# Hybrid recurrent decoder step: projections as one plain fp32 matmul per 128 rows in place of three float32r products

## The chip, the cores and the metric

The kernel runs on one core of one Trainium2 chip. The metric is the device time of one execution in microseconds (us); lower is better. A core has five engines that run their own queues in order: PE (TensorE, matmuls; its weight loads are listed apart as PEld), DVE (VectorE), ACT (ScalarE), POOL (GpSimd) and SP (SyncE), which here issues the DMAs.

## The reference

One layer (model width 1024) serves a prompt of 1024 tokens and eight sample sequences of one token each. What matters here are the two large projections around the mixers:

```python
h = rms_norm(x, norm_g)
proj = jnp.matmul(h, w_in).astype(F32)       # 1032 rows, 30 tiles of 128 columns
...                                          # GLA, S5, gated delta net, RWKV-7, each times a SiLU gate
mixed = jnp.concatenate([o_gla, o_s5, o_gdn, o_rwkv], axis=-1)
out = jnp.matmul(mixed, w_out.astype(F32))   # 1032 rows, 8 tiles of 128 columns
return x + out.astype(x.dtype), ...
```

The final RMSNorm follows. The mixers are recurrences over the tokens, worked out in chunks; the projected columns feed them, and all of it is float32.

## The kernel before

The tokens are handled in two halves: 512 prompt tokens (half 0), and 512 prompt tokens with the 8 sample tokens (half 1, 520 columns in two pieces of 260). `norm_x` normalizes the rows of a half, transposes them on PE and keeps them as two float32r tiles: `xhi`, the rounded value, and `xlo`, what the rounding left. `stream` computes 128 projected columns: eight weight slabs of 128x128 are brought in two transfers into `wr`, and `wsplit` makes the same two parts of them, `wh` on ACT (L265) and `wl` on POOL (L266). Then each slab is multiplied three times into one PSUM tile `psp` (L277): `xhi` by `wh`, `xlo` by `wh`, `xhi` by `wl`. A caller's `evac` takes `psp` away on ACT or DVE. `proj` calls `stream` for the 30 input tiles of each half; `tail` does so for the 8 output tiles (L277 with `ohi` and `olo`), then transposes (L1301), adds x (L1303) and normalizes.

The work between is that of the units named in a list `ORDER`: RWKV (R, chain of chunk states at L483), gated delta net (D, chain at L689), GLA (L, L819), S5 (W for its block matrices, S), and gates (g). The inverses that R and D need are a chain of 31 pairs of small DVE operations (L307, L309). L1184 is the one other large weight product, of S5's gate (`yt` by `wglu`), in plain float32. A scheduler sets the order on every engine from `ORDER` and a table of priorities, so that projections stand in PE's queue between the steps of the recurrences. Raw weights have three buffers, `wh` and `wl` two each; `xhi` and `xlo` (and `ohi`, `olo`, which use the same space) have one.

Of the kernel before, what the change touches and what calls it, by code (L numbers as in the profile page):

```python
# [9 lines left out]
F32R = mybir.dt.float32r  # L10
# [6 lines left out]
T = 1024  # L17
# [7 lines left out]
NB = dict(ta=9, pr=11, on=3, gp=8, sh=2, kA=6, XT=2, Gt=5, s8=4, ss=4, wr=3, wh=2, wl=2, d1=1, LT=1, DT=2, DP=1, d2=2, Dn=2, w8=2, rf=1,  # L25
# [5 lines left out]
           rU="V", dU="V", fg="V", la="V", tlo="V", cv0="V")  # L31
# [32 lines left out]
def trunk(ctx: ExitStack, tc: tile.TileContext, I, O):  # L64
# [20 lines left out]
    def cload(name, shape):  # L85
        """A block of columns of the constants that one transfer brings."""
        b, o, p = CONST[name]
        if b not in blobs:
            blobs[b] = const.tile([128, CONST_W[b]], F32, name="const" + b)
            SP.dma_start(out=blobs[b], in_=I["const" + b])  # L90
        v = blobs[b][:p, o:o + math.prod(shape[1:])]
        return v.rearrange("p (a b) -> p a b", a=shape[1]) if len(shape) == 3 else v

    def late(ins, after):
        """Schedule ins, which nothing else holds back, only when after has been issued: its tile waits for its turn."""
# [18 lines left out]
    def tt(name, out, a, b, op=ALU.mult):  # L114
        """out = a op b on the engine that ENG names."""
# [14 lines left out]
    def load_x(h, after=None):  # L130
        """The rows of a half and the gains of its norm."""
# [11 lines left out]
    # ------------------------------------------------------------ constants  # L143
# [29 lines left out]
    # what is carried from the first half of the sequence to the second  # L173
# [12 lines left out]
    # ------------------------------------------------------------ small pieces  # L186
    def rsqrt_small(y, m, t):
        """y = m ** -0.5 for small tiles: ln and exp, then a Newton step."""
# [7 lines left out]
    def sig_arg(e, x, bias=None):  # L196
        """e = x (+ bias), bounded where exp(-x) would run out of the range of Ln: 1 / (1 + e^43) < 2^-62."""
# [5 lines left out]
    def sig_chain(e, *outs):  # L203
        """sigmoid(e) to each (out, columns of e)."""
# [8 lines left out]
    def sample_bc(src):  # L213
        """[128 (h, v), 8] -> PSUM [128 (h, any), 8, 64]: each head's values along the free dim."""
# [6 lines left out]
    def mat_vec(S, col):  # L221
        """sum over keys i of S[(h, i), b, v] * col[(h, i), b], on all partitions of the head."""
# [13 lines left out]
    # ------------------------------------------------------------ projection stream  # L236
    def norm_x(h, tiles):
        """RMSNorm of a half, transposed, in two parts that float32r holds exactly."""
        hi = xp.tile([128, 8, NH], F32R, tag="hi", name="xhi")
        lo = xp.tile([128, 8, NH], F32R, tag="lo", name="xlo")  # L240
        ngb = tiles[0]
        for i in range(5 if h else 4):
# [9 lines left out]
            for b in range(2):  # L252
# [3 lines left out]
                A.copy(hi[:, 4 * b:4 * b + 4, c:c + n], pt[:, :, :n])  # L256
                V.tensor_tensor(lo[:, 4 * b:4 * b + 4, c:c + n], pt[:, :, :n], hi[:, 4 * b:4 * b + 4, c:c + n], ALU.subtract)  # L257
        XS[h] = dict(hi=hi, lo=lo, n=NH if h else HALF)

    def wsplit(src):  # L260
        raw = wst.tile([128, 4, 128], F32, tag="wr", bufs=NB["wr"], name="wr")
        SP.dma_start(out=raw, in_=src)
        hi = wst.tile([128, 4, 128], F32R, tag="wh", bufs=NB["wh"], name="wh")
        lo = wst.tile([128, 4, 128], F32R, tag="wl", bufs=NB["wl"], name="wl")
        A.copy(hi, raw)  # L265
        G.tensor_tensor(lo, raw, hi, ALU.subtract)  # L266
        return hi, lo

    def stream(wsrc, evac):
        """evac(PSUM [128, m], c0, m) for the columns of (128 columns of w).T @ x."""  # L270
        wt = [wsplit(wsrc[:, 4 * q:4 * q + 4, :]) for q in range(2)]
        for c0, m in X["pieces"] or pieces(X["n"]):
            p = ps_p.tile([128, 512], F32, tag="p", name="psp")
            for k in range(8):
                hi, lo = wt[k // 4]
                for s, (w, x) in enumerate(((hi, X["hi"]), (hi, X["lo"]), (lo, X["hi"]))):
                    X["mm"] = PE.matmul(p[:, :m], w[:, k % 4, :], x[:, k, c0:c0 + m], start=(k == 0 and s == 0), stop=(k == 7 and s == 2))  # L277
# [8 lines left out]
    # ------------------------------------------------------------ inverses of unit lower triangular matrices  # L286
    def inverse(Ga, XT, after):
        """XT[64 p + s, k, t] = ((I - L) ** -1)[t, s] for the 16 strictly lower L[t, s] = Ga[p][..][s, k, t] of a unit;
        p is the parity of a chunk and k = (pair of chunks, head), in one or two tiles."""
# [39 lines left out]
    # pairs of chunks are kept as (first of one, second of one, second of the other, first of the other)  # L329
# [10 lines left out]
    # ------------------------------------------------------------ RWKV-7  # L340
# [164 lines left out]
    # ------------------------------------------------------------ gated delta net  # L505
# [10 lines left out]
    def small_in(h):  # L516
        """low-rank gate of GLA (rows 0:16), a (32:36) and b (64:68) of the delta net."""
# [56 lines left out]
    def conv_in(h, ct, raw):  # L574
        """causal convolution over 4 tokens and SiLU of one column tile of q, k, v."""
# [25 lines left out]
    def l2(x, out, scale, eps):  # L601
        """out = x * (scale * (sum over the head of x * x) + eps) ** -0.5"""
# [105 lines left out]
    # ------------------------------------------------------------ gated linear attention  # L708
# [6 lines left out]
    def gla_unit(h, pair, sm):  # L715
# [55 lines left out]
        # q.k of a token with itself, and of the second of two with the first, by rows of the first  # L771
# [738 lines left out]
```

## Time and profile before

| | |
|---|---|
| three runs | 1075.30, 1083.88, 1084.38 us; median 1083.88 |
| profiled execution, first to last instruction (span) | 1069.0 us |
| PE busy | 928.3 us, 87% of the span, 5994 matmul records |
| DVE busy | 704.2 us, 66% |
| ACT busy | 459.6 us, 43% |
| POOL busy | 395.3 us, 37% |
| mean granted clock of PE | 0.858 of full speed |

The page gives the span of the profiled execution and no time of its own beside it; the three runs lie 6.3 to 15.4 us above that span. Busy time is the time in which at least one record of an engine runs. Matmul records overlap, so the pace of a stream is read from the starts of its records, not from their durations. A plain float32 matmul of full width leaves two records, a float32r one leaves one.

### The profile page before, as it was taken

How to read it: one execution, taken by the hardware profiler on the slowest of the kernel's cores; microseconds unless marked ns; L12 is line 12 of the kernel's file. 1: busy time of each engine (PE TensorE's matmuls, PEld its weight loads, DVE VectorE, ACT ScalarE, POOL GpSimd, SP SyncE). 2: the span in 40 equal slices, each digit the busy share in tenths (PEclk: the TensorE clock that was granted, in tenths of full speed). 3: DMA queues.
4: the chain of work that ended last, by engine and by line, in shares of the span. 5: the costliest groups of instructions: out<-in, count | busy, mean ns of one | idle time of the engine just before them, and what ended most of it. 6: DMA issues, size and time to landing. Idle time of an engine off the chain costs nothing. (4 is left out here: it accounts for less than half of the span.)

```text
span 1069.0 us, 16993 instructions
## 1 busy us (share of the span) xinstructions
PE 928.3 (87%) x5994; PEld 762.7 (71%) x5994; DVE 704.2 (66%) x1871; ACT 459.6 (43%) x1033; POOL 395.3 (37%) x434
## 2 busy tenths in 40 slices
PE   3899889979999788897989898988989989769794
PEld 3676657658777576797788767677868958658694
DVE  8528884668648864736578989979875366553514
ACT  4355544332644343522753454643235235162634
POOL 2788654531321441133363403125326312313231
PEclk9999979876898666798999889888888569869898
DMA  7133414210211132224223223311112014612532
GB/s 235 50 127 106 115 59 111 71 54 21 74 49 43 46 93 81 81 79 148 69 85 97 77 76 83 92 47 50 53 59 71 22 66 126 212 49 79 183 128 86
DMA packets 76804, 92.23 MB, mean 86 GB/s; under 512 B 41400, under 2 KB 43584, under 8 KB 76720
## 3 DMA queue, kind: packets, MB, share of 16 engines
q1 hardware_dynamic: 76720, 91.16, 27.2%
q8 instruction: 47, 0.77, 0.3%
q14 instruction: 37, 0.30, 0.1%
HBM read 74.38 MB, written 14.62 MB: 83 GB/s over the span
## 5 line engine op out<-in xcount | busy, mean ns | idle before, releaser
L266 POOL TENSOR_TENSOR wl<-wr,wh 128x512 fp32r<-128x512 f32 x152 | 204.6, 1348 | 420.5 <-ACT wh L265 403.6
L277 PE MATMUL psp<-xhi,wh 128*128 128x260 f32 (+2 forms) x728 | 262.2, 361 | 10.7 <-DVE rx L355 6.5
L277 PE MATMUL psp<-xhi,wl 128*128 128x260 f32 (+2 forms) x728 | 256.3, 355 | 5.2 <-POOL wl L266 5.0
L277 PE MATMUL psp<-xlo,wh 128*128 128x260 f32 (+2 forms) x728 | 253.3, 349 | 0.8 <-DVE xlo L257 0.8
L277 PEld LDWEIGHTS psp<-xhi,wh 128*128 128x128 f32 x728 | 153.2, 210 | 33.8 <-issue 12.8
L277 PEld LDWEIGHTS psp<-xhi,wl 128*128 128x128 f32 x728 | 151.2, 209 | 25.4 <-POOL wl L266 7.4
L265 ACT CAST wh<-wr 128x512 fp32r<-128x512 f32 x152 | 93.7, 618 | 172.3 <-PE psp L277 92.9
L277 PEld LDWEIGHTS psp<-xlo,wh 128*128 128x128 f32 x728 | 153.2, 211 | 16.7 <-issue 3.8
L307 DVE TENSOR_TENSOR DP<-DT,LT 128x60 f32<-128x60 f32 (+24 forms) x248 | 81.9, 330 | 12.5 <-DMA XT<-d 3.1
L309 DVE TENSOR_TENSOR DT<-DT,DP 128x60 f32<-128x60 f32 (+24 forms) x248 | 73.8, 297 | 6.1
L277 PE MATMUL psp<-ohi,wh 128*128 128x260 f32 (+1 forms) x192 | 65.5, 342 | 5.4 <-ACT yT L1295 3.5
L277 PE MATMUL psp<-olo,wh 128*128 128x260 f32 (+1 forms) x192 | 64.0, 334 | 1.8 <-DVE olo L116 1.8
L277 PE MATMUL psp<-ohi,wl 128*128 128x260 f32 (+1 forms) x192 | 62.9, 334 | 0.0
L1303 DVE TENSOR_TENSOR xf<-psb,xf 128x128 f32<-128x128 f32 x64 | 14.5, 282 | 49.6 <-PE psb L1301 41.3
L277 PEld LDWEIGHTS psp<-ohi,wh 128*128 128x128 f32 x192 | 37.7, 197 | 8.5 <-ACT yT L1295 3.9
L762 PE MATMUL psb<-W 64*128 64x64 f32 x256 | 40.7, 331 | 1.8 <-DVE DT L309 1.8
L112 ACT ACTIVATE eg<-eg 128x260 f32<-128x260 f32 (+1 forms) x72 | 34.0, 486 | 18.2 <-DVE eg L199 17.4
L277 PEld LDWEIGHTS psp<-olo,wh 128*128 128x128 f32 x192 | 37.7, 196 | 4.6 <-DVE olo L116 2.1
L762 PEld LDWEIGHTS psb<-W 64*128 64x128 f32 x256 | 36.4, 237 | 5.7 <-issue 3.1
L277 PEld LDWEIGHTS psp<-ohi,wl 128*128 128x128 f32 x192 | 37.0, 195 | 2.4 <-POOL wl L266 0.2
L116 POOL TENSOR_TENSOR df<-cum 128x256 f32<-128x256 f32 x48 | 30.8, 663 | 17.2 <-DVE cum L737 15.2
L483 PE MATMUL psc<-UV,Gt 64*128 64x64 f32 (+1 forms) x256 | 35.6, 288 | 0.6 <-ACT UV L476 0.6
(423 smaller groups left out, 1862.4 us busy)
## 6 DMA issues: line engine op xcount, KB each, us to landing
wr<-in_wct SPq DMA_DIRECT2D x120, 256.0 KB
wr<-in_wo SPq DMA_DIRECT2D x32, 256.0 KB
xn<-in_x SPq DMA_DIRECT2D x8, 512.0 KB
LT<-d SPq DMA_DIRECT2D x32, 128.0 KB
xf<-in_x SPq DMA_DIRECT2D x8, 512.0 KB
out_y<-xf SPq DMA_DIRECT2D x8, 512.0 KB
dgp<-gp SPq DMA_DIRECT2D x8, 256.0 KB
Gml<-dG SPq DMA_DIRECT2D x4, 512.0 KB
```

The lines of the kernel that those rows point to most:

```text
L112: A.activation(out, in_, func, bias=bias, scale=scale, **kw)
L116: return (G if ENG[name] == "G" else V).tensor_tensor(out, a, b, op)
L265: A.copy(hi, raw)
L266: G.tensor_tensor(lo, raw, hi, ALU.subtract)
L277: X["mm"] = PE.matmul(p[:, :m], w[:, k % 4, :], x[:, k, c0:c0 + m], start=(k == 0 and s == 0), stop=(k == 7 and s == 2))
L307: V.tensor_tensor(tp[:, :m, :w], DT[:, :m, j:j + 1].to_broadcast([128, m, w]), LT[:, j:j + 1, j + 1:32].to_broadcast([128, m, w]), ALU.mult)
L309: V.tensor_tensor(DT[:, :m, j + 1:32], DT[:, :m, j + 1:32], tp[:, :m, :w], ALU.add)
L483: PE.matmul(o, l, r, start=start, stop=True, skip_group_check=True)
L762: PE.matmul(pg[:, c, :], W[HS[e], t], W[HS[e], t].rearrange("p (b f s) -> p f b s", f=2, s=s)[:, 1], start=True, stop=True)
L1303: V.tensor_tensor(xf[j][:, cols], pt[:, j, :], xf[j][:, cols], ALU.add)
```

## The change

The split is taken out everywhere. `norm_x` writes the transposed rows once, as float32 (`xT`); `wload` brings the weights and PE reads them where they land; `stream` makes one float32 matmul per slab (L268 in the changed kernel, where lines stand 9 to 11 earlier). `tail` copies half 1's gates into one float32 tile `oT`, and loads half 0's there by DMA directly. Raw weights get six buffers, and `xT`/`oT` two. All other lines of the difference are comments.

```diff
-NB = dict(..., wr=3, wh=2, wl=2, ...
+NB = dict(..., wr=6, xT=2, ...
...
     def norm_x(h, tiles):
-        hi = xp.tile([128, 8, NH], F32R, tag="hi", name="xhi")
-        lo = xp.tile([128, 8, NH], F32R, tag="lo", name="xlo")
+        xt_ = xp.tile([128, 8, NH], F32, tag="x", bufs=NB["xT"], name="xT")
...
-                A.copy(hi[:, 4 * b:4 * b + 4, c:c + n], pt[:, :, :n])
-                V.tensor_tensor(lo[:, 4 * b:4 * b + 4, c:c + n], pt[:, :, :n], hi[:, 4 * b:4 * b + 4, c:c + n], ALU.subtract)
-        XS[h] = dict(hi=hi, lo=lo, n=NH if h else HALF)
-
-    def wsplit(src):
-        raw = wst.tile([128, 4, 128], F32, tag="wr", bufs=NB["wr"], name="wr")
-        SP.dma_start(out=raw, in_=src)
-        hi = wst.tile([128, 4, 128], F32R, tag="wh", bufs=NB["wh"], name="wh")
-        lo = wst.tile([128, 4, 128], F32R, tag="wl", bufs=NB["wl"], name="wl")
-        A.copy(hi, raw)
-        G.tensor_tensor(lo, raw, hi, ALU.subtract)
-        return hi, lo
+                A.copy(xt_[:, 4 * b:4 * b + 4, c:c + n], pt[:, :, :n])
+        XS[h] = dict(x=xt_, n=NH if h else HALF)
+
+    def wload(src):
+        w = wst.tile([128, 4, 128], F32, tag="wr", bufs=NB["wr"], name="wr")
+        SP.dma_start(out=w, in_=src)
+        return w
...
             for k in range(8):
-                hi, lo = wt[k // 4]
-                for s, (w, x) in enumerate(((hi, X["hi"]), (hi, X["lo"]), (lo, X["hi"]))):
-                    X["mm"] = PE.matmul(p[:, :m], w[:, k % 4, :], x[:, k, c0:c0 + m], start=(k == 0 and s == 0), stop=(k == 7 and s == 2))
+                X["mm"] = PE.matmul(p[:, :m], wt[k // 4][:, k % 4, :], X["x"][:, k, c0:c0 + m], start=(k == 0), stop=(k == 7))
...
     def tail(h):
-        hi = xp.tile([128, 8, NH], F32R, tag="hi", name="ohi")
-        lo = xp.tile([128, 8, NH], F32R, tag="lo", name="olo")
+        ot = xp.tile([128, 8, NH], F32, tag="x", bufs=NB["xT"], name="oT")
...
-            if not h:
-                p = prt("gpl")
-                SP.dma_start(out=p[:, :n], in_=dgp[k])
-            A.copy(hi[:, k, :n], p[:, :n])
-            tt("tlo", lo[:, k, :n], p[:, :n], hi[:, k, :n], ALU.subtract)
-        X.update(hi=hi, lo=lo, n=n)
+            if h:
+                A.copy(ot[:, k, :n], p[:, :n])
+            else:
+                SP.dma_start(out=ot[:, k, :n], in_=dgp[k])
+        X.update(x=ot, n=n)
```

The scheduler writes a new order for every engine. Three places show it. The first is ACT's queue at the start of half 0, before:

```order
L256 CAST xhi<-psb 128x4x128 x2
L112 ACTIVATE ss<-ss 128x1 x2
L265 CAST wh<-wr 128x512 x2
L256 CAST xhi<-psb 128x4x128 x4
L112 ACTIVATE sh<-psp,constA 128x256
```

and after:

```order
L254 COPY xT<-psb 128x4x128 x2
L111 ACTIVATE ss<-ss 128x1 x2
L254 COPY xT<-psb 128x4x128 x2
L111 ACTIVATE sh<-psp,constA 128x256
L254 COPY xT<-psb 128x4x128 x4
```

The casts of weights (`wh`) are gone, and the first evacuation of a projection (`sh`, from `psp`) stands ahead of the last four copies.

The second is PE's queue among the first chunk steps of an RWKV chain in half 0 (`UV`, `Gt`, `Bn`, `AR`, `XT` and `state` are the chain's tiles), before:

```order
L277 MATMUL psp<-xlo,wh 128x512
L277 MATMUL psp<-xhi,wl 128x512
L277 MATMUL psp<-xhi,wh 128x512
L728 MATMUL psb<-sm,constB 128x512
L483 MATMUL psc<-UV,Bn 128x128
L483 MATMUL psc<-UV,Gt 64x64 x2
```

and after:

```order
L474 MATMUL psc<-r,XT 64x64 x2
L474 MATMUL psc<-UV,Gt 128x64 x4
L474 MATMUL psc<-UV,Bn 128x128
L474 MATMUL psc<-UV,Gt 64x64 x2
L474 MATMUL psc<-state_116,AR 128x128
L461 MATMUL psc<-constA,BK 128x128 x2
```

Projections that stood between the first chunk steps now stand elsewhere: there is no L268 among them.

The third is PE's queue in the last output tiles of half 1, before:

```order
L277 MATMUL psp<-olo,wh 128x260
L1301 MATMUL psb<-constA,yT 128x128 x2
L1306 MATMUL psb<-constA,yT 8x128
L277 MATMUL psp<-ohi,wh 128x260
L277 MATMUL psp<-olo,wh 128x260
L277 MATMUL psp<-ohi,wl 128x260
```

and after:

```order
L268 MATMUL psp<-oT,wr 128x260 x12
L1290 MATMUL psb<-constA,yT 128x128 x2
L268 MATMUL psp<-oT,wr 128x260 x4
L1290 MATMUL psb<-constA,yT 128x128 x2
L1295 MATMUL psb<-constA,yT 8x128
```

The transposes of one tile still stand among the products of the next; 16 float32 matmuls now make a tile, where 48 float32r ones did.

## Rows read from the trace of the kernel before

**Rows 1.** The page, part 1: busy time, share of the span and records.

```profile
PE 928.3 (87%) x5994; PEld 762.7 (71%) x5994; DVE 704.2 (66%) x1871; ACT 459.6 (43%) x1033; POOL 395.3 (37%) x434
```

**Rows 2.** Windows by stage: length, busy time per engine, granted clock, DMA share, GB/s.

```profile
27.00:200.00 173.00, 157.37 (x760) 113.96 (x759) 105.64 (x230) 77.23 (x147) 111.19 (x122) 0.90 0.30 93
200.00:460.00 260.00, 229.65 (x1434) 182.29 (x1433) 176.42 (x497) 107.86 (x250) 76.72 (x85) 0.78 0.20 63
460.00:600.00 140.00, 124.79 (x891) 111.82 (x890) 94.76 (x191) 63.68 (x133) 60.48 (x74) 0.95 0.30 92
600.00:918.00 318.00, 290.96 (x2123) 243.38 (x2122) 239.25 (x645) 135.84 (x336) 98.43 (x100) 0.85 0.23 69
952.00:1050.00 98.00, 90.84 (x578) 81.19 (x579) 40.42 (x136) 37.98 (x87) 34.45 (x26) 0.94 0.31 111
```

**Rows 3.** Waits of PE: who waited for whom, us in total, times, longest.

```profile
PE psc L689 <- DVE U L122: 9.2, 7, 2.6
PE psb L255 <- DVE xlo L257: 9.1, 5, 4.2
PE psp L277 <- POOL wl L266: 5.0, 5, 2.9
```

**Rows 4.** Groups by line and shape: count, busy us, mean ns, idle before.

```profile
L266 POOL TENSOR_TENSOR wl<-wr,wh 128x512 fp32r<-128x512 f32 x152 | 204.6, 1348 | 420.5 <-ACT wh L265 403.6 <-PE psp L277 13.1 <-PE psb L1086 2.1
L277 PE MATMUL psp<-xhi,wh 128*128 128x260 f32 x480 | 153.2, 320 | 8.3 <-DVE rx L355 6.5 <-DVE gp L1218 1.0 <-ACT shout L359 0.8
L277 PEld LDWEIGHTS psp<-xhi,wh 128*128 128x128 f32 x728 | 153.2, 210 | 33.8 <-issue 12.8 <-DVE gp L1218 3.7 <-ACT wh L265 3.0
L277 PE MATMUL psp<-xhi,wh 128*128 128x512 f32 x232 | 103.6, 446 | 2.4 <-ACT wh L265 1.5 <-DVE gp L1218 0.9
L265 ACT CAST wh<-wr 128x512 fp32r<-128x512 f32 x152 | 93.7, 618 | 172.3 <-PE psp L277 92.9 <-issue 66.8 <-POOL sh L350 5.9
L277 PE MATMUL psp<-ohi,wh 128*128 128x260 f32 x128 | 38.2, 300 | 2.0 <-ACT ohi L1266 2.0
L277 PE MATMUL psp<-ohi,wh 128*128 128x512 f32 x64 | 27.3, 426 | 3.5 <-ACT yT L1295 3.5
```

**Rows 5.** Timeline of PE, float32r projections: start us, us; first and last of a run.

```profile
58.94 0.39 PE L277 MATMUL psp<-xlo,wh 128*128 128x512 f32 x1
...
60.80 0.40 PE L277 MATMUL psp<-xhi,wh 128*128 128x512 f32 x1
...
518.71 0.29 PE L277 MATMUL psp<-xhi,wl 128*128 128x260 f32 x1
...
519.66 0.28 PE L277 MATMUL psp<-xlo,wh 128*128 128x260 f32 x1
...
702.35 0.42 PE L277 MATMUL psp<-xlo,wh 128*128 128x260 f32 x1
...
703.87 0.42 PE L277 MATMUL psp<-xhi,wl 128*128 128x260 f32 x1
```

**Rows 6.** Line L1184, plain float32: its records, and two merged stretches of the timeline.

```profile
L1184 PE MATMUL psb<-yt,wglu x24: 382/592/803, 519.8 to 948.0; 128*128 128x260 f32 x16, 128*128 128x512 f32 x8
...
519.79 1.45 PE L1184 MATMUL psb<-yt,wglu 128*128 128x512 f32 x3
...
947.08 1.26 PE L1184 MATMUL psb<-yt,wglu 128*128 128x260 f32 x5
```

**Rows 7.** The inverses on DVE: duration min/median/max of L307, and its group on the page.

```profile
L307 DVE TENSOR_TENSOR DP<-DT,LT x248: 136/220/1317, 119.6 to 757.7; 128x60 f32<-128x60 f32 x12, 128x54 f32<-128x54 f32 x8, 128x66 f32<-128x66 f32 x8, 128x28 f32<-128x28 f32 x8
...
L307 DVE TENSOR_TENSOR DP<-DT,LT 128x60 f32<-128x60 f32 (+24 forms) x248 | 81.9, 330 | 12.5 <-DMA XT<-d 3.1
```

More of the change, by code (lines that the diff above doesn't have):

```diff
@@ L9 @@
 F32 = mybir.dt.float32
-F32R = mybir.dt.float32r
 I32 = mybir.dt.int32
@@ L24 @@
 NH = HALF + NS
-NB = dict(ta=9, pr=11, on=3, gp=8, sh=2, kA=6, XT=2, Gt=5, s8=4, ss=4, wr=3, wh=2, wl=2, d1=1, LT=1, DT=2, DP=1, d2=2, Dn=2, w8=2, rf=1,
+NB = dict(ta=9, pr=11, on=3, gp=8, sh=2, kA=6, XT=2, Gt=5, s8=4, ss=4, wr=6, xT=2, d1=1, LT=1, DT=2, DP=1, d2=2, Dn=2, w8=2, rf=1,
           fx=3, bv=2, Bn=2, UV=2, r=3, dr=2, gcn=2, ben=2, kdn=2, U=3, at=2, s5i=1, s5h=3, nst=2, psp=2, psb=2, psc=4)
@@ L30 @@
            glu="V", g5="V", cvm="V", l2="V", sgl1="V", sgl2="V", lw0="V", lw1="G", ld0="G", ld1="G", lqk="V", rS="A", rr="V",
-           rU="V", dU="V", fg="V", la="V", tlo="V", cv0="V")
+           rU="V", dU="V", fg="V", la="V", cv0="V")
 PRI = {"R2": 4000, "D2": 1000, "R3": 4000, "D3": 4000, "L1": 2000, "R1": 600, "L0": 100, "L2": 600, "D0": 300, "D1": 1000}
@@ L255, in norm_x @@
                     PE.transpose(pt[:, k, :n], xn[:n, (4 * b + k) * 128:(4 * b + k + 1) * 128], ident[:n, :n])
-                A.copy(hi[:, 4 * b:4 * b + 4, c:c + n], pt[:, :, :n])
-                V.tensor_tensor(lo[:, 4 * b:4 * b + 4, c:c + n], pt[:, :, :n], hi[:, 4 * b:4 * b + 4, c:c + n], ALU.subtract)
-        XS[h] = dict(hi=hi, lo=lo, n=NH if h else HALF)
-    def wsplit(src):
-        raw = wst.tile([128, 4, 128], F32, tag="wr", bufs=NB["wr"], name="wr")
-        SP.dma_start(out=raw, in_=src)
-        hi = wst.tile([128, 4, 128], F32R, tag="wh", bufs=NB["wh"], name="wh")
-        lo = wst.tile([128, 4, 128], F32R, tag="wl", bufs=NB["wl"], name="wl")
-        A.copy(hi, raw)
-        G.tensor_tensor(lo, raw, hi, ALU.subtract)
-        return hi, lo
+                A.copy(xt_[:, 4 * b:4 * b + 4, c:c + n], pt[:, :, :n])
[4 more added lines that the diff above has]
+        return w
     def stream(wsrc, evac):
-        wt = [wsplit(wsrc[:, 4 * q:4 * q + 4, :]) for q in range(2)]
+        wt = [wload(wsrc[:, 4 * q:4 * q + 4, :]) for q in range(2)]
         for c0, m in X["pieces"] or pieces(X["n"]):
```

## The prediction

> **What bounds the kernel now.** I read the page's totals first: PE is busy 87% of the span, DVE 66%, ACT 43%, POOL 37% [rows 1]. Since the chip's stages differ, the stages come next: in each of them PE is the busiest engine, with 88 to 93% [rows 2]. From 952 us on, where the output tiles run, DVE, ACT and POOL are busy for two fifths or less, and PE alone sets the end. In the two stretches of recurrences (200 to 460 and 600 to 918 us) DVE is busy 68% and 75%, and there PE's clock is lowest, 0.78 and 0.85. A busy PE is not yet a paced one, so I looked at who PE waits for: the largest single entry is 9.2 us, steps of the delta net that wait for DVE; the split appears with 9.1 us at the transposes (`xlo` had to empty a PSUM tile) and 5.0 us at the products (`wl`) [rows 3]. So the split is mostly hidden: POOL spends 204.6 us on it and ACT 93.7 us, but POOL idles 420.5 us before these operations [rows 4]. PE is the bound, and what it is given to do decides.
>
> **PE's own work.** The projections have 232 + 64 = 296 slabs of 512 columns and 480 + 128 = 608 of 260, and 16 of 256 remain of the first column tile [rows 4] (each slab makes one record of a group). The pace before is read from starts: 512 columns from 58.94 to 60.80 us in eight steps, 0.2325 us each; 260 columns from 518.71 to 519.66 in eight, 0.119 each [rows 5]. A slab takes three, 0.697 and 0.356 us. The pace after has an example in the same trace, L1184, which is plain float32 with weights of the same size. It made 24 records for 12 matmuls (four of 512, eight of 260, by the code), so a matmul is two records. Three of 512 columns last 1.45 us and the last of them 0.592, so they start 0.429 apart; five of 260 last 1.26 with 0.382 for the last, 0.219 apart [rows 6]. A slab then takes 0.858 and 0.439 us. The difference is +0.161 and +0.083 us a slab at full clock: 296 x 0.161 = 47.7, 608 x 0.083 = 50.5, and 16 x 0.08 = 1.3, together **+99 us**.
>
> Where the clock is at half speed it costs more, since there 260 float32r columns take 0.217 us (702.35 to 703.87 in seven steps) [rows 5], three of them 0.651, against 2 x 0.438 = 0.876 if float32 doubles: +0.225 in place of +0.083; the 512 ones +0.43 in place of +0.16. The stages' clocks [rows 2] say that time at half speed is 20% (27 to 200), 44%, 10%, 30% and 12%; I estimate that a seventh of the slabs meet it, as the projections are densest where the clock is high. That adds 0.143 x (608 x 0.142 + 296 x 0.27) = 24 us: at most **+123** with the clocks as they are. I take +115.
>
> **What the split gives back.** Three terms, all out of PE's idle time, which is 15.6 + 30.4 + 15.2 + 27.0 = 88 us from 27 to 918 us and 7 us from 952 to 1050 (length less PE busy [rows 2]).
> First, PE's direct waits for the split, 9.1 + 5.0 us [rows 3], and some small ones in the last tail where the only `ohi` and `olo` are refilled. The transposes still wait for the copy to `xT`, and the first products for weights from DRAM, so not all of it comes back: -10, between 0 and -18.
> Second, faster steps of the recurrences. POOL's split is half of POOL's work, 204.6 of 395.3 us [rows 1, 4], and operations on DVE take longer at times: L307 has a median of 220 ns, a mean of 330 and a longest of 1317 [rows 7]. If what lies over the median comes from POOL working at the same time, and half of that is the split, then L307 and its twin L309 (as many) return some 248 x 0.11 x 2 x 0.5 = 27 us of DVE time. ACT's queue loses its 152 casts, which stood ahead of evacuations, as its order at the start shows. What part lies on a path that PE waits for is unknown: all of it -45, none 0; I take -20, since the recurrences' waits are spread over many short entries like the 9.2 us one.
> Third, longer projections fill gaps in which PE now idles before a chunk step. That can't exceed the idle time left, 95 - 30 = 65; the order after has fewer projections between the first RWKV steps, so less is filled there. I take -25, between 0 and -65.
> The sum is 115 - 55 = +60, against a span of 1069.0. Around the span lie 15 us in the median of the runs, which the change doesn't touch: 1069 + 60 + 15 = 1144. Against the median of 1083.88 that is 5.6% slower.
>
> Edits costed at nothing: the six `wr` buffers (PE must now read a buffer before SP can refill it, but three raw and two split ones before held five of these half tiles, and six do now); the direct loads of `oT`, which are the same eight transfers as `gpl`; the transfer of weights, whose bytes stay. Cover for all three is PE's own longer work, 0.858 us a slab where a half tile holds four. If a load queued behind a blocked `wr` transfer on SP came late, the stretch of S5 loads before 952 us would show it, by some us.
>
> **Rivals.**
> *The recurrences wait behind longer products.* PE's queue is in order, and one slab holds it 0.86 us instead of 0.23 us per record before. If nothing of the idle time comes back, +123: 1207 us. For it: the idle entries are short and many [rows 3], so a gap rarely fits a slab. Against it: three float32r records of one slab mostly stood together already.
> *DVE, POOL and ACT were the bound after all.* Then the 95 us of idle time and the stalls in it go, and 99 - 95 = +4: about 1088, no change. For it: DVE at 75% in the longest stretch [rows 2]. Against it: PE's idle time there is 27 of 318 us.
> *The clock rises* (the other side). Each slab now holds PE longer, so the stretches at 0.78 and 0.85 might be granted full speed. Time at half speed is twice the missing clock: 35 + 114 + 14 + 95 + 12 = 270 us [rows 2]. Full speed halves PE's share of it, 0.9 x 270 / 2 = 121 us. It outweighs the +60 once more than half of it turns; if three quarters do, 1144 - 91 = 1053. For it: the densest projections, 460 to 600 us, have 0.95. Against it: the low stretches are those of chunk steps, which change little, and the order after puts fewer projections among the first of them. The Trainium skill (TensorE: Matmul & The Clock Gate, "What's actually happening") says that the slow clock is the default and that activity releases it. The rows agree as far as they go; no row shows float32 streams releasing it sooner than float32r ones.
> *Weight loads set the pace.* The loads fall from 2760 to 1840, as a float32 matmul loads twice. A load lasts 210 ns [rows 4]; were PE's time their sum, 920 x 0.21 = 193 us would go, and 1084 - 193 = 891 come out. Against it: 260 columns start 0.119 us apart, in less than one load's duration [rows 5], so loads overlap and columns set the pace. The Trainium skill (Trainium Kernel Development and Optimization, "Performance Expectations") holds the busy share of LDWEIGHTS, not that of matmuls, to be the measure of how near PE is to its limit; by that rule PE has room at 71%, and this rival would be the likeliest. The row on 260 columns speaks against it here.
> *The change isn't what it says*, if a large float32 product ran in one record: PE would get 0.43 instead of 0.70 us a slab, and lose about 165 us, 920 or so. L1184's 24 records speak against it [rows 6].
>
> **How the numbers follow.** The forecast (+20 to +100) has a chance of 0.64, waiting chains 0.18, no change 0.09 (two thirds of it within 1%), the clock 0.05, weight loads 0.02, one record 0.02. A change of 1% is about what a measurement of this kernel can tell from none. Faster by over 1%: 0.05 + 0.02 + 0.02 = 0.09; within 1%: 0.06; slower: 0.64 + 0.18 + 0.03 = 0.85. The predicted time is 1144. The range leaves out the faster cases (0.09), the cases of no change (about 0.08) and little above: 1097, where a quarter of the idle time beyond my value is also filled, to 1202, just short of nothing coming back.
>
> **What would show it.** In the changed profile each slab of L268 should leave two records, 0.429 or 0.219 us apart at full clock, and the final output tiles should take 16 x 0.083 = 1.3 us more each. POOL's busy time should fall to about 190 us and ACT's to about 350, L307's mean towards 220 ns. PE busy should rise by 70 to 115 us and its idle time shrink by some 50. The forecast is wrong if L268 shows one record or another spacing, if the mean clock moves by more than 0.04, or if PE's waits for DVE grow.

## The result, and the profile after

The changed kernel takes 1179.72 us in the median of four runs (1165.44 to 1182.75); the kernel before took 1084.13 us in four runs beside it (1075.30 to 1085.26). The ratio is 1.099, with an interval of 1.085 to 1.114: slower by 10%, where 1144 us (5.6%) was forecast. The profiled execution after took 1182.29 us for a span of 1180.5. So 1.8 us lie around the span. The execution profiled before, with its span of 1069.0, was shorter than the median of its kernel; there were no 15 us around it.

The page of the kernel after, part 1, answers to [rows 1]:

```profile
PE 1051.5 (89%) x5074; PEld 724.8 (61%) x5074; DVE 615.2 (52%) x1837; ACT 370.2 (31%) x873; POOL 178.8 (15%) x282
```

DVE, ACT and POOL lost 89, 89 and 217 us, as a kernel without the split must; PE gained 123. PE's time without any record fell from 1069.0 - 928.3 = 141 us to 1180.5 - 1051.5 = 129. So of all that the three engines gained, 12 us came back as less idle time of PE, and the span grew by nearly all of PE's own 123.

The groups by line and shape after answer to [rows 4] (count, busy us, mean ns, idle before):

```profile
L268 PE MATMUL psp<-xT,wr 128*128 128x260 f32 x960 | 247.8, 412 | 7.8 <-DVE rx L346 4.4 <-ACT xT L254 1.0 <-ACT raw L560 0.9
L268 PE MATMUL psp<-xT,wr 128*128 128x512 f32 x464 | 223.2, 635 | 0.8 <-ACT l L111 0.7
L268 PE MATMUL psp<-oT,wr 128*128 128x260 f32 x256 | 60.6, 389 | 0.0
L268 PE MATMUL psp<-oT,wr 128*128 128x512 f32 x128 | 58.1, 599 | 3.6 <-ACT yT L1284 3.6
```

464 records are 2 x 232, and 960 are 2 x 480: a slab is one float32 matmul and two records, as L1184 said [rows 6]. The pace is in the timeline (start us, duration us, records merged in one line):

```profile
45.39 36.32 PE L268 MATMUL psp<-xT,wr 128*128 128x512 f32 x84
...
1161.25 3.67 PE L268 MATMUL psp<-oT,wr 128*128 128x260 f32 x16
```

The last record of the first stretch lasts 0.592 us, so its 84 start (36.32 - 0.592)/83 = 0.430 us apart in the mean; over the whole trace the median is 0.429 where the clock is full. Of 260 columns the last lasts 0.382, and 16 start (3.67 - 0.382)/15 = 0.219 apart. Both are the forecast's numbers. At half speed the medians are 0.853 and 0.433 us, so float32 doubles there, as the forecast supposed.

Windows by stage after answer to [rows 2] (length, busy time of PE, PEld, DVE, ACT and POOL, granted clock, DMA share, GB/s):

```profile
27.00:200.00 173.00, 164.78 (x551) 78.01 (x550) 85.72 (x191) 53.85 (x97) 61.06 (x92) 0.98 0.34 100
200.00:460.00 260.00, 239.98 (x1270) 157.01 (x1269) 145.75 (x458) 87.20 (x214) 34.31 (x48) 0.73 0.17 51
460.00:600.00 140.00, 120.79 (x599) 94.94 (x598) 49.63 (x112) 40.25 (x93) 15.45 (x35) 0.92 0.29 91
600.00:918.00 318.00, 290.53 (x1594) 221.82 (x1594) 212.28 (x611) 104.60 (x255) 52.33 (x77) 0.80 0.21 60
918.00:1050.00 132.00, 111.28 (x571) 85.27 (x569) 55.27 (x156) 39.68 (x103) 10.80 (x8) 0.66 0.25 78
1050.00:1160.00 110.00, 104.67 (x411) 72.17 (x412) 33.47 (x127) 22.19 (x61) 0.00 (x0) 0.97 0.28 96
```

The work lies later than before, so these rows and those of before are not the same work; what they show is the clock. Where projections are dense it is 0.92 to 0.98; in the chunk steps it is 0.66 to 0.80, lower than the 0.78 and 0.85 of before. Over the span the mean fell from 0.858 to 0.828: time at half speed, twice the missing clock times the span, rose from 304 to 406 us. The same windows for line L268 alone (PE busy, PEld busy, clock, DMA share, GB/s) show where:

```profile
880.00:920.00 40.00, 21.60 (x89) 16.45 (x88) 0.88 0.13 40
920.00:960.00 40.00, 0.00 (x0) 0.00 (x0) 0.54 0.18 63
960.00:1000.00 40.00, 26.04 (x64) 12.72 (x64) 0.84 0.13 40
1000.00:1040.00 40.00, 0.00 (x0) 0.00 (x0) 0.59 0.51 155
```

Two stretches of 40 us hold no projection at all, and there the clock is 0.54 and 0.59, near the lower of its two levels (half speed, 0.5). Their neighbours with projections have 0.88 and 0.84. Before, the stretch of this kind with the fewest projections (of line L277, same columns) still holds some:

```profile
920.00:960.00 40.00, 8.21 (x24) 6.33 (x24) 0.66 0.42 142
```

PE isn't idle in such a stretch. Of the 54 us around the first one it is busy for 48.69, with 284 records and no projection among them (columns as in the windows by stage):

```profile
907.00:961.00 54.00, 48.69 (x284) 37.83 (x282) 30.89 (x90) 17.35 (x51) 7.28 (x9) 0.58 0.15 53
```

In the whole trace before, one gap between projections is longer than 25 us (35 us, at a clock of 0.68). After, there are five, of 27 to 59 us, at 0.58 to 0.71.

Who PE waited for after, answering to [rows 3] (us in total, times, longest):

```profile
PE psb L1175 <- DVE yt L115: 10.9, 2, 6.6
PE psb L253 <- DVE xn L249: 10.5, 3, 9.0
PE psb L225 <- DVE mv L223: 9.2, 3, 4.3
PE psc L474 <- DVE state L490: 8.0, 7, 1.7
PE psc L474 <- DVE UV L121: 7.9, 12, 1.9
```

The entries of `xlo` and `wl`, 14.1 us together, are gone. The longest are now S5's gate (L1175), the transposes of the normalized rows (L253) and steps of the recurrences, which all wait for DVE; each of these five was there before too, and those of S5 and of `mv` (L225) doubled, from 4.3 and 4.4 us. All of PE's waits together fell from 127 to 115 us, those for DVE from 91 to 85.

Last, the inverses, answering to [rows 7] (duration min/median/max of the line, then its group on the page):

```profile
L298 DVE TENSOR_TENSOR DP<-DT,LT x248: 154/215/1273, 120.9 to 814.8; 128x60 f32<-128x60 f32 x12, 128x54 f32<-128x54 f32 x8, 128x66 f32<-128x66 f32 x8, 128x28 f32<-128x28 f32 x8
```

```profile
L298 DVE TENSOR_TENSOR DP<-DT,LT 128x60 f32<-128x60 f32 (+24 forms) x248 | 63.6, 257 | 21.9 <-DMA LT<-d 15.2
```

The mean fell from 330 to 257 ns at nearly the same median, 18 us for this line. Its idle time before rose by 9 us: half of the gain turned into waiting.

### The profile page after: what moved, and what is told of

It is laid out like the page before. It is cut to its first block, busy times and chain, and to the rows that moved or that the text cites. A ratio compares the mean times of both kernels' runs of the same rounds, so it can differ in the third digit from the quotient of the medians.

```text
span 1180.5 us, 14644 instructions
## 1 busy us (share of the span) xinstructions
PE 1051.5 (89%) x5074; PEld 724.8 (61%) x5074; DVE 615.2 (52%) x1837; ACT 370.2 (31%) x873; POOL 178.8 (15%) x282
## 4 chain that ended last, share of the span: by engine, by line
PE 70%; DVE 15%; DMA 5%; ACT 5%; issue 2%; SPq 2%; POOL 0%; ACTq 0%; DVEq 0%; POOLq 0%
PE psp L268 40%; PE psc L474 5%; PE psc L680 4%; PE psb L753 3%; DVE DT L300 2%; DVE DP L298 2%; PE psb L225 1%; PE psc L317 1%; PE psb L774 1%; PE psb L431 1%; PE psc L810 1%; PE psc L314 1%; DMA LT<-d 1%; DMA d<-DT 1%; PE psb L1175 1%
## 5 line engine op out<-in xcount | busy, mean ns | idle before, releaser
L268 PE MATMUL psp<-xT,wr 128*128 128x260 f32 (+2 forms) x1456 | 480.3, 484 | 8.8 <-DVE rx L346 4.4
L268 PEld LDWEIGHTS psp<-xT,wr 128*128 128x128 f32 x1456 | 289.6, 205 | 159.0 <-issue 109.2
L268 PE MATMUL psp<-oT,wr 128*128 128x260 f32 (+1 forms) x384 | 118.6, 459 | 3.6 <-ACT yT L1284 3.6
L268 PEld LDWEIGHTS psp<-oT,wr 128*128 128x128 f32 x384 | 71.6, 193 | 35.7 <-issue 24.4
L298 DVE TENSOR_TENSOR DP<-DT,LT 128x60 f32<-128x60 f32 (+24 forms) x248 | 63.6, 257 | 21.9 <-DMA LT<-d 15.2
L474 PEld LDWEIGHTS psc<-UV,Gt 64*128 64x128 f32 (+1 forms) x256 | 31.8, 212 | 15.3 <-issue 7.1
L693 DVE SCALAR_TENSOR_TENSOR state<-state,egb,psc 64x64 f32<-64x64 f32 x64 | 17.9, 279 | 40.8 <-PE psc L680 39.6
L577 DVE SCALAR_TENSOR_TENSOR acc<-raw,constA,acc 128x512 f32<-128x512 f32 x36 | 26.6, 768 | 9.9 <-ACT acc L111 9.8
L111 ACT ACTIVATE df<-df 128x512 f32<-128x512 f32 x24 | 15.1, 629 | 43.1 <-POOL df L115 43.1
L253 PE MATMUL psb<-constA,xn 128*128 128x128 f32 (+1 forms) x72 | 13.6, 351 | 14.6 <-DVE xn L249 10.5
```

Source lines behind the costliest of these rows:

```text
L111: A.activation(out, in_, func, bias=bias, scale=scale, **kw)
L253: PE.transpose(pt[:, k, :n], xn[:n, (4 * b + k) * 128:(4 * b + k + 1) * 128], ident[:n, :n])
L268: X["mm"] = PE.matmul(p[:, :m], wt[k // 4][:, k % 4, :], X["x"][:, k, c0:c0 + m], start=(k == 0), stop=(k == 7))
L298: V.tensor_tensor(tp[:, :m, :w], DT[:, :m, j:j + 1].to_broadcast([128, m, w]), LT[:, j:j + 1, j + 1:32].to_broadcast([128, m, w]), ALU.mult)
L474: PE.matmul(o, l, r, start=start, stop=True, skip_group_check=True)
L577: V.scalar_tensor_tensor(acc[:, :HALF], raw[:, j:j + HALF], w(j), acc[:, :HALF], ALU.mult, ALU.add)
```

## The experiments

The theory at the start of the experiments was that the columns' +99 us come out in the time one for one, that the split gives little back because it was hidden, and that the rest is the lower clock and the buffers. The rivals were that the split's removal gives much and something else in the change takes it away, or that gaps fill. In the comparisons below, runs made together share those of the kernel before (1078.73, 1072.57, 1076.23 and 1075.76 us in the median).

### The products alone

The kernel before, with its float32r tiles made float32 and the first of the three products kept. The first part of each operand is then the operand itself, so the product is whole; the copies and subtractions of the split are still done.

```diff
-F32R = mybir.dt.float32r
+F32R = mybir.dt.float32
...
-                for s, (w, x) in enumerate(((hi, X["hi"]), (hi, X["lo"]), (lo, X["hi"]))):
-                    X["mm"] = PE.matmul(p[:, :m], w[:, k % 4, :], x[:, k, c0:c0 + m], start=(k == 0 and s == 0), stop=(k == 7 and s == 2))
+                X["mm"] = PE.matmul(p[:, :m], hi[:, k % 4, :], X["hi"][:, k, c0:c0 + m], start=(k == 0), stop=(k == 7))
```

> The kernel before with one edit: the tiles of the split are plain float32 and only the first product (hi by hi) is made; the copies on ACT and the subtractions on POOL and DVE stay as work without use, and so do the old buffers. Theory A (the columns cost what was computed, and the new order that the scheduler makes for float32 products leaves chunk steps without projections, which then run at half clock): the order of this kernel is like that of the changed one, so mean clock 0.82 to 0.84 and stretches without projections of over 7 us sum to about 420 us; time 1180 to 1215, the relief of the split being small. Theory B (taking the split away is what loosens the projections and lowers the clock): clock 0.85 to 0.86, stretches of about 250 us, time 1084 + 100 = 1170 to 1185.

Measured: 1182.73 us against 1078.73, a ratio of 1.099 (1.090 to 1.108), +104 us. The mean granted clock was 0.860. Its page, part 1:

```profile
PE 1035.1 (88%) x5074; PEld 703.3 (59%) x5074; DVE 692.3 (59%) x1871; ACT 459.5 (39%) x1033; POOL 385.2 (33%) x434
```

The +99 us of columns come out whole: PE's time without a record is 1182.3 - 1035.1 = 147 us, against 141 before, so longer projections fill no gaps. The clock is that of before, as theory B had it, so it isn't the longer products that lower it; the stretches without projections sum to 355 us, between the two theories. And the products alone, with all of the split still there, take as long as the whole change.

### The split's second parts alone

The other half: the kernel before with its three float32r products, but `xlo`, `wl` and `olo` never made; the three products all take the first parts. This output leaves out the corrections.

```diff
-        lo = wst.tile([128, 4, 128], F32R, tag="wl", bufs=NB["wl"], name="wl")
...
-        G.tensor_tensor(lo, raw, hi, ALU.subtract)
-        return hi, lo
+        return hi, hi
```

> The kernel before without the second parts: no subtraction on POOL and DVE; the cast on ACT stays (float32r needs it), and the three products are made of the first parts alone, so PE has the same columns as before and the output leaves out the corrections. It prices the relief of the split (the term that I put at -10 -20 and, filled gaps aside, no more than -65). Theory A: order and clock stay near those before (0.85 to 0.87), DVE busy falls by some 60 to 80 us, time 1045 to 1080. Theory B: with the split's brake gone the chunk steps lose their cover, clock 0.83 or less, time 1084 or more.

Measured: 1050.61 us against 1078.73, a ratio of 0.974 (0.967 to 0.982), -28 us. Its page, part 1:

```profile
PE 930.3 (89%) x5994; PEld 767.7 (74%) x5994; DVE 617.3 (59%) x1837; ACT 456.3 (44%) x1033; POOL 186.8 (18%) x282
```

DVE lost 87 us and POOL 209, and 28 came out. It came out of PE's time without a record, 141 us before and 111 here, while PE's busy time rose by 2. The trace parts it: PE's waits for `xlo`, `olo` and `wl` were 17 us before and are gone, and its other waits together fell from 110 to 98. The mean granted clock fell from 0.858 to 0.839; what that took back, the run doesn't show by itself.

### Keeping TensorE busy in the chunk steps

The changed kernel with 192 more matmuls of 128 columns in the chunk steps of RWKV and the delta net, three in each, into columns of PSUM that are not read.

```diff
+            def keep():
+                for _ in range(KEEP):
+                    PE.matmul(pc[:, 384:512], ident, ident, start=False, stop=True, skip_group_check=True)
```

> The changed kernel with three added matmuls (identity by identity, 128 columns of float32, into an unused part of the PSUM tile) in each of the 64 chunk steps of RWKV and the delta net, right behind the step's own products: 192 matmuls, about 41 us of PE time at full clock, in places where PE works alone on small products. Theory A (half clock in the steps follows from PE's little activity there): the time at half clock falls by 60 us or more of 371, the mean clock rises to 0.85 or above, and the added 41 us cost less than 25: 1160 to 1205. Rival (the clock doesn't follow what is done in the steps): clock stays at 0.83, time 1215 to 1240.

Measured: 1216.63 us, a ratio to before of 1.129 (1.120 to 1.137), against 1.099 for the change. The granted clock rose from 0.828 to 0.858, as theory A had it, and the time came out in the rival's range: the added matmuls cost more than the clock gave. Their two groups of 192 records were busy 53.3 and 52.5 us. The Trainium skill (TensorE: Matmul & The Clock Gate, "What's actually happening") says that activity releases the slow clock, and this run agrees, with the two clocks above. It also shows that work for its own sake doesn't pay here.

### The buffers

The changed kernel with the buffer counts of before (`wr` 3, `xT` 1), then each count alone, then two raw buffers.

```diff
-NB = dict(..., wr=6, xT=2, ...
+NB = dict(..., wr=3, xT=1, ...
```

> The changed kernel with three weight buffers in place of six and one buffer of transposed rows in place of two, as before the change. If the looser buffers let the projections run ahead and so cost clock: 1150 to 1170 and clock 0.845 or above. If the buffers hide transfers: 1190 to 1210 with more waits of PE for weights. Theory A: 1170 to 1195, no difference that can be told.

> The changed kernel with three weight buffers in place of six (the two buffers of transposed rows stay). With both old buffer counts the changed kernel took 1164 in place of 1180. If the weight buffers are what lets projections run ahead of the chunk steps: 1160 to 1170, stretches without projections near the 383 us seen with both. If it is the second buffer of rows: 1175 to 1190, near 426 us.

> The changed kernel with one buffer of transposed rows in place of two (six weight buffers stay). The counterpart: 1175 to 1190 if the weight buffers matter, 1160 to 1170 if the buffer of rows does.

> The changed kernel with two weight buffers and one buffer of rows: a projection's weights can only be fetched as the last one's are read, a stronger brake than before the change. Theory A (projections that run ahead leave the chunk steps alone at half clock): stretches without projections under 360 us, the excess of the small products at half clock under 75 us (113 in the changed kernel, 83 with the old buffers), clock 0.86 or more; the time 1145 to 1165, if PE's waits for weights don't eat it. Rival (the buffers matter through transfers alone): PE waits for weights, 1180 to 1210.

Measured, beside the change:

```
version       wr  xT   median us   ratio to before          clock
the change     6   2   1179.72     1.099 (1.085 to 1.114)   0.828
wr alone       3   2   1177.69     1.101 (1.094 to 1.108)   0.853
xT alone       6   1   1161.25     1.085 (1.079 to 1.092)   0.851
both           3   1   1163.83     1.080 (1.073 to 1.087)   0.856
two raw        2   1   1145.92     1.072 (1.065 to 1.079)   0.859
```

The six raw buffers do nothing that can be told, with one `xT` or with two. The second buffer of transposed rows costs 1.4 points with six raw buffers and 2.1 with three, though a buffer more can only save waits for one. (The two versions of 1177.69 and 1161.25 us ran together; they differ in both counts.) The clock differs most, in both pairs, in the stage from 918 to 1050 us. It is 0.66 there in the change and 0.74 with `wr` alone changed, against 0.81 and 0.82 in the two versions with one `xT`. The window with `wr` alone changed, and that with `xT` alone changed:

```profile
918.00:1050.00 132.00, 104.99 (x580) 76.55 (x579) 62.57 (x181) 41.80 (x113) 10.98 (x8) 0.74 0.26 82
```

```profile
918.00:1050.00 132.00, 108.23 (x586) 73.00 (x586) 60.66 (x193) 39.98 (x111) 8.10 (x5) 0.81 0.31 102
```

A clock lower by 0.15 (0.81 to 0.66) in 132 us is 0.15 x 2 x 132 = 40 us more at half speed, which cost a PE that is busy 84% about half of that, 17 us: about as much as the difference between the change and `xT` alone. Between the other two the clock doesn't explain it. It differs by 0.08 in this stage, but from 600 to 918 us the slower version has the higher clock (0.84 against 0.81), and over the span it is 0.853 against 0.856. There PE's waits are 7 us longer (135 against 128), and the rest of the 2.1 points has no cause that was found. In both pairs PE's order, by the tiles of its records, is the same for 1806 of 5074 and then parts. So the cost lies most likely in the order that the scheduler writes when it has the second buffer, and not in a buffer waited for; for the pair with three raw buffers this is argued, not shown. The run with two raw buffers makes PE wait for weights (us, times, longest), and is still the fastest of the five:

```profile
PE psp L268 <- DMA wr<-in_wct: 12.9, 5, 5.8
```

With fewer buffers the projections are spread further over the chunk steps. Gaps of over 7 us between the end of one projection record and the start of the next, summed over the trace, are 426 us in the change, 383 with the counts of before and 314 with two raw buffers. With `wr` alone and `xT` alone changed they are 393 and 398: this sum, by which the forecast meant to tell the two apart, doesn't.

### Less work for POOL, paid with DMA

The kernel before, storing the weights' second parts in DRAM in half 0 and loading them in half 1 in place of the second subtraction.

```diff
-        G.tensor_tensor(lo, raw, hi, ALU.subtract)
+        if key in dlo:
+            SP.dma_start(out=lo.bitcast(F32), in_=dlo[key])
+        else:
+            G.tensor_tensor(lo, raw, hi, ALU.subtract)
...
+                SP.dma_start(out=dlo[key], in_=lo.bitcast(F32))
```

> The kernel before, float32r with the split; the second parts of the weights, once made for half 0, are written to DRAM and read back for half 1, so POOL makes 76 subtractions in place of 152, and the transfers grow by some 38 MB. Leaving the subtractions out altogether gave 28 us of 1079. If POOL's work costs through DVE and the recurrences: 8 to 20 us faster, 1059 to 1071. If the added transfers queue ahead of others on SP: 1079 or slower.

Measured: 1088.90 us against 1072.57, a ratio of 1.016 (1.009 to 1.023). POOL fell from 395.3 to 287.3 us and DVE from 704.2 to 664.6, and the time rose. The run doesn't tell how much faster recurrence steps are worth, since its products wait for the new transfers:

```profile
PE psp L285 <- DMA wl<-dlo: 6.9, 5, 3.6
```

### The output tiles alone

The kernel before, with one float32 tile and one float32 matmul per slab in the 16 output tiles only.

```diff
+            for k in range(8):
+                X["mm"] = PE.matmul(p[:, :m], wt[k // 4][:, k % 4, :], X["x"][:, k, c0:c0 + m], start=(k == 0), stop=(k == 7))
...
-            stream(I["wo"][m], evac)
+            stream32(I["wo"][m], evac)
```

> The kernel before, with float32 only in the 16 output tiles at the end (one float32 tile in the space of ohi and olo; everything ahead of them as before). Theory A (in a stretch where PE alone sets the end, every added column comes out in the time): 64 slabs x 0.161 + 128 x 0.083 = 21 us more on PE, less up to 7 us of waits for ohi and olo, so 14 to 21 us above before, a ratio of 1.013 to 1.020. Rival (gaps between the tiles take up the longer products): at most 5 us above before, ratio 1.005 or less.

Measured: 1094.36 us against 1076.23, a ratio of 1.021 (1.013 to 1.029). The four runs range from 1086.46 to 1106.17; that is +14 us by the median without the longest, +18 with it and +23 by the ratio, where 21 were worked out for the columns. The rival, that the gaps between the tiles take them up, falls. Its page has the same two records per slab:

```profile
L278 PE MATMUL psp<-oT,wr 128*128 128x260 f32 (+1 forms) x384 | 123.7, 475 | 4.2 <-ACT yT L1305 3.3
```

### The list of units alone

The changed kernel with nothing but its list `ORDER` altered, so that PE's queue has fewer long runs of chunk steps without a projection.

```diff
-ORDER = ("x W t W m W R0 g6 R0 D0 W W M W D0 D1 R1 W R0 R1 R0 L0 ...
-         "L1 x' g7 g1 g4 S t' R1' R1' m' R0' g1 R1' g3 M' R1' R0' g2 ... D1' g4' g6' D0' "
-         "L0' L1' L1' D1' g2' g7' g0' L0' D1' g6' g4' L0' S' g5' g3' S' g3' g0' g2' g5' g1' T T'")
+ORDER = ("x W t W m W R0 R0 D0 W W M W D0 D1 R1 W R0 R1 g6 R0 L0 ...
+         "L1 x' g7 g1 g4 S t' R1' R1' m' R0' R1' g3 g1 M' R1' R0' g2 ... D1' g4' g6' D0' "
+         "L0' L1' L1' D1' g2' g7' g0' L0' g4' D1' g6' L0' g1' S' g5' g3' S' g3' g0' g2' g5' T T'")
```

> The changed kernel with nothing but its list ORDER altered: a few gate units and others stand at other places, so that PE's queue has fewer long runs of chunk steps without a projection. Theory A (such runs are where the clock falls and the chunk steps pay for it): mean clock above 0.84 and 5 to 20 us below the changed kernel, a ratio of 1.08 to 1.095 to before. Rival (the runs are a sign and no cause; the recurrences' own waits set the time): the same 1.10 within 0.5 points, clock about 0.83 to 0.85.

Measured: 1159.88 us against 1076.23, a ratio of 1.078 (1.073 to 1.084), 2 points below the change; the clock is 0.854 in place of 0.828:

```profile
core 0: 1156.4 us, clock 0.854
```

Every engine has as many records as in the change. So 2 of the change's 10 points are the order in which its work stands, and they come back together with the clock.

### Both at once

The altered list and the two raw buffers with one of transposed rows (`wr` 2, `xT` 1).

> The changed kernel with the altered list ORDER and with two raw buffers and one of transposed rows. Each edit alone gave 2 to 3 points back (ratios 1.078 and 1.072 instead of 1.099). Theory A (both act through the same thing, the placement of projections among the chunk steps, and what is left is the products' own columns, some 9 points less the split's 2): 1.065 to 1.08, no better than the tight buffers alone. Rival (two separate costs, which add up): 1.045 to 1.06.

Measured: 1148.28 us against 1075.76, a ratio of 1.068 (1.061 to 1.075), with the highest clock of all the profiles:

```profile
core 0: 1142.0 us, clock 0.876
```

The two edits don't add up: one alone gave 1.072, both give 1.068, and the intervals overlap. No other order was tried. What is left, some 7 points, is close to the columns' 99 us less what the split is worth: 28 us on the kernel before (71/1076 = 6.6%), 19 on the float32 kernel (80/1076 = 7.4%).

### One product in place of three

The kernel without second parts, with one float32r product per slab. The output leaves out the corrections.

```diff
-                for s, (w, x) in enumerate(((hi, X["hi"]), (hi, X["lo"]), (lo, X["hi"]))):
-                    X["mm"] = PE.matmul(p[:, :m], w[:, k % 4, :], x[:, k, c0:c0 + m], start=(k == 0 and s == 0), stop=(k == 7 and s == 2))
+                X["mm"] = PE.matmul(p[:, :m], hi[:, k % 4, :], X["hi"][:, k, c0:c0 + m], start=(k == 0), stop=(k == 7))
```

> The kernel before with one float32r product per slab of the rounded parts alone; the second parts, and their two products, are left out, and the output with them lacks the corrections. Against the run without second parts but with three products (1050.6 us) two thirds of the projections' columns go, some 283 us at full clock. Theory A (PE's columns set the time one for one, in both directions): 770 to 820 us. Rival (behind PE stands the next bound, the recurrences' chains on DVE, busy about 617 us in that run, and a lower clock): 850 to 950 us, with PE busy below 75% and its waits for DVE several times as long.

Measured: 920.48 us against 1076.23, a ratio of 0.856 (0.852 to 0.860). Against the run with three products of the same parts (1050.61), some 283 us of columns at full clock went and 130 came out. The mean granted clock was 0.703. Its page, part 1:

```profile
PE 712.8 (78%) x4154; PEld 551.9 (60%) x4154; DVE 616.8 (67%) x1837; ACT 451.1 (49%) x1033; POOL 185.0 (20%) x282
```

Its longest waits of PE (us, times, longest):

```profile
PE psb L1143 <- DMA dTl<-dT: 14.8, 1, 14.8
PE psb L406 <- ACT ta L112: 11.8, 3, 6.3
PE psb L1294 <- ACT yT L1288: 11.0, 4, 5.3
PE psc L684 <- DVE state L697: 10.9, 12, 1.8
```

Columns added come out one for one, columns taken away less than half. The rival's time was right and its signs were not quite: PE is still busy 78%, not below 75, and its waits for DVE are 106 us in place of the 63 with three products, not several times as long. Two things took the rest. PE's time without a record rose from 1042 - 930 = 111 us in the run with three products to 919 - 713 = 206, spread over many waits; and time at half speed rose from 2 x 0.161 x 1042 = 335 us to 2 x 0.297 x 919 = 546.

## Why the prediction came out as it did

The sign and the range were right, the value 36 us too low. The measured time lies nearer to the price of a rival, waiting chains (1207), than to the forecast; the range held it because it reached nearly up to that price. By its own steps:

**PE's own work** was right. The +99 us rest on 0.429 and 0.219 us a record, which the pace showed; they were measured at +104 us in time by the products alone, and at +14 to +23 for a computed 21 in the output tiles. That PE is the bound, and that what it is given to do decides, held too: the experiment with the products alone is as slow as the whole change.

**The half clock** was looked for in the wrong place. The forecast added 16 us for slabs that meet it and took the clocks "as they are". Worked out from the starts of all records, by clock, the projections lost about 46 us to the half clock before and 36 after, so no more is lost there. The other matmuls lost about 67 us before and 113 after, since the time at half speed grew by 102 us. (Taking half of all PE time at half speed instead gives 53 and 38, and 74 and 131: other sizes, the same directions.) This fits the windows, where stretches without L268 have 0.54 and 0.59. The rival of a rising clock had the right lever with the wrong sign; the prediction named a move of more than 0.04 as its failure, and the move was 0.030. Its other sign of failure, that PE's waits for DVE grow, did not come either (91 to 85 us).

**What the split gives back** is the step that failed most: -55 was forecast. With the products' cost taken out, the second parts are worth -28 us on the kernel before, and on the float32 kernel with the buffers of before the whole split, with the direct loads of `oT`, is worth 1182.73 - 1163.83 = 19 us. Its three terms fared differently. The direct waits went as said, 17 us with `olo`, where -10 was forecast. The faster steps are real (L298's mean of 257 ns in place of 330), but by the run without second parts PE's other waits fell by 12 us, where -20 was forecast. The gaps that longer projections fill, -25, gave nothing: the products alone came out at +104 for +99, and PE's idle time was 147 us there in place of 141. So PE's idle time shrank by 12 us after the change and not by 50; its busy time rose by 123, not by 70 to 115. It was the rival of waiting chains that had said "a gap rarely fits a slab"; it held for this one term, though its price of 1207 was too high.

**Edits costed at nothing** were not all free: the buffers, with the order that the scheduler writes for them, cost 1.9 points by the ratios of the change (1.085 to 1.114) and of the version with the counts of before (1.073 to 1.087). This part was not in any rival. The direct loads of `oT` were not tried alone; nothing in the profile after shows PE waiting for them.

**Around the span** 15 us were added that aren't there: 1.8 us lie around it, and the other 13 are how far the profiled execution was ahead of the median one. For a forecast of a median they were harmless, since they only moved the start of the sum to the median; the 36 us are the error of the +60.

**Two smaller slips.** The largest single wait of PE before is not the delta net's 9.2 us but the transposes' 9.6 for `xn`, also for DVE, which changes nothing in the sum. And the lower end of the range, 1097, doesn't follow from its reason: a quarter of the 40 us of idle time that the forecast left over would be 10 us below 1144.

**The measured terms** are +104 from the products, -19 from the split and +1.9% of 1084 = 21 from the buffers and their order, +106; the medians differ by 95.6, and the interval of the ratio allows 92 to 123. These are steps from one kernel to the next, so that they meet the whole is no check on them; what each step is made of is shown by its own run alone.

**The other rivals** fall. DVE, POOL and ACT were not the bound: taking 87 us from DVE and 209 from POOL gave 28. Weight loads don't set the pace: their records fell by 920 and their busy share from 71% to 61%, while the time rose by 10%. The Trainium skill (Trainium Kernel Development and Optimization, "Performance Expectations") names the busy share of LDWEIGHTS, beside MFU (the share of the peak arithmetic rate), as a good measure of how near a kernel is to the limit; by that share the kernel would now be further from it. Here it fell because there are fewer loads of nearly the same length (205 ns in the mean against 210) and each is followed by more streaming, 0.429 us in place of 0.2325, while added columns still cost their full time.

**What stays open.** That the missing projections cause the low clock in the chunk steps is supported by the added matmuls (the clock rose by 0.030) and by the list alone (by 0.026), but the sum of gaps doesn't order all versions: the kernel before has 246 us of them at 0.858, the products alone 355 at 0.860, the list alone 391 at 0.854. What else enters wasn't found. Nor was it settled why the scheduler, given a second `xT`, writes a worse order, or which of the change's clock loss belongs to which edit: without second parts, but with the old buffers, the clock fell to 0.839, and without any split and with the old buffers it was 0.856.

## What to carry to other kernels

Where one engine is the bound, cost its columns from the starts of its records and expect added ones to come out whole; don't credit gaps with taking them up unless a row shows a gap as long as the new piece. Work taken off engines that are hidden gives back only the waits that it caused, and the bound's clock may then give some of that away. When a scheduler writes the order, a changed buffer count is a changed program: run the edit with the old counts too, which gave some 2 of 10 points here. And look at the clock where PE works on small matmuls alone; a PE that is busy 90% can still be at half speed.

## What the runs showed of the hardware

- At full clock a float32 matmul of 128x128 weights is two records of 0.429 us for 512 columns (0.219 for 260), so 0.858 us; three float32r products of the same slab are 3 x 0.2325 = 0.697 us. Three products of the one kind cost less than one of the other.
- The granted clock moves with what stands between the chunk steps: with the same work in another order it was 0.854 in place of 0.828, and with a third of the projections' columns 0.703. From 907 to 961 us of the changed kernel PE was busy for 48.69 of 54 us, without a projection, at a clock of 0.58.
- Within one kernel the runs differ with the clock: the four of the change took 1165.44 us at 0.844, 1177.15 at 0.835, 1182.29 at 0.828 and 1182.75 at 0.827, some 1 us for 0.001. That is what half speed costs a PE that is busy 89%: 0.001 x 2 x 1180 x 0.89 / 2 = 1.05 us.
- DVE's small operations got shorter as POOL's work went. The mean of the inverses' first line (L307 before) was 330 ns with POOL busy 395 us, 277 with 287 us (weights' second parts loaded), 261 with 187 us (none made) and 257 with 179 us (the change), with medians of 220 before and 215 after. Its twin (L309) had 297, 308, 255 and 259 ns. ACT was as busy without second parts as before (456 and 460 us), so it isn't ACT's work that made the difference.
